# Projecting v of the four recurrent heads in one pass, tokens on partitions

## The chip, the cores and the metric

The kernel runs on one core of one Trainium2 chip. A core has the matrix engine TensorE (PE; the profile lists its weight loads separately as PEld), VectorE (DVE), ScalarE (ACT), GpSimd (POOL) and SyncE (SP, which here only issues transfers), 16 DMA engines, an on-chip memory of 128 partitions and eight PSUM banks into which PE writes. The metric is the device time of one execution in microseconds (us).

## The reference

The program is one layer of an encoder with 1024 tokens and 1024 channels: a mixer, a cross attention over 256 memory tokens, a mixture of 16 experts, and a final normalisation. The change lies in the mixer:

```
h = RMSNorm(x);  P = h @ W_in          # W_in is 1024 x 3584: seven slots of 512 columns
cb, cc, cx, hq, hf, hi, hg = split(P, 7)
y_a = cb * conv3_causal(cc * cx)
f = lb + (1 - lb) * sigmoid(hf);  k = (1 - lb) * sigmoid(-hf);  q = hq;  v = hi   # 4 heads of 128
S_t = diag(f_t) S_{t-1} + k_t v_t^T;   o_t = S_t^T q_t                            # per head
y_b = RMSNorm_per_head(o) * silu(hg)
x = x + concat(y_a, y_b) @ W_out
```

v is the slot `hi`: 512 columns, 128 for each of the four heads.

## The kernel before, in words

All products of this part are done in three matmuls on operands split into a high and a low part (`products`, L257 to L259: high by high, high by low, low by high), each with a 128x128 stationary operand and 512 streamed columns. The input x lies transposed (channels on partitions) as eight pairs `xh[k]`, `xl[k]` of 128x1024. W_in comes as 28 blocks of 128 columns; each block is a tile of 512 KB that holds the eight 128x128 pieces of its contraction.

A stream `W` brings the weights. It loads blocks in the order of `SEQ` through SP (L199) into free slots, and a generator `run` splits them: the high part by a cast on ACT (L163), the low part by a subtraction on DVE (L169). At most `W.limit` split blocks are ready ahead of their use. `W.get` forces a block that isn't ready. There are 48 slots of 128x1024, given out first in, first out.

`project(i, evac)` takes one block as the stationary operand and streams x: for each half of the tokens 8 triples of matmuls into one bank, which `evac` reads. Its result has the block's 128 channels on partitions and tokens along the free axis. After each triple it calls `advance(648)`. This is how the order of the program is written: `advance` moves a clock by 648 and runs the next step of every side generator whose due time has come; a generator gives its next due time by `yield`. `finish(s)` runs all remaining steps of a side at once. The steps are emitted in this order, and the compiler's scheduler, which has a cost model of its own, may start a later instruction first when the earlier one isn't ready by its model. On the chip each engine then runs its list in order.

The order is: `conv(0)` (blocks CC, CX, CB); then for each head h the inputs `hgrn_inputs(h)` with four projections HF, HI, HG, HQ, beside which the recurrent part `hgrn(h-1)` of the head before runs as a side; then `conv(1)` with three projections, beside `hgrn(3)`; then `conv(2)`, `conv(3)`, and the rest of the layer. After each `hgrn_inputs` and after `conv(1)` a `finish` completes the running head.

`hgrn` needs v with tokens on partitions. HI gives it with channels on partitions, copied out by ACT (L481). So `hgrn` begins with two steps: four PE transposes each (L264, called at L502), after which ACT copies four 128x128 tiles with the token's RMS factor `rx` as scale (L504). Then come the diagonal scores (L519), q times f (L525), seven levels of a doubling scheme (PE at L538 or L544; DVE at L547, L548, L550, L552), two steps that transpose k, two for the states (L581, L588), two for the outputs (L602, L604, squares on ACT at L608), the per-head RMS factor on POOL (`rstd_cols`, L180 and L181), its product with the output on DVE (L615), two steps that transpose the output (L264) and multiply by the gate on DVE (L623), and a store.

At the start `begin` computes `rx` and, by matmuls of ones with diagonal tiles (L387 on DVE, L390 on PE), a tile `rbc` of it along the free axis. Squares of x run on ACT (L372).

Of the kernel before, what the change touches and what calls it, by code (L numbers as in the profile page):

```python
# [14 lines left out]
AF = mybir.ActivationFunctionType  # L15
# [9 lines left out]
P = 128  # L25
T = 1024
D = 1024
NT = T // P
ND = D // P
HALF = 512  # L30
M = 256
NH = 4
# [53 lines left out]
def block_kernel(ctx: ExitStack, tc: tile.TileContext, A):  # L86
    nc = tc.nc
    act, dve, pool, pe, sp = nc.scalar, nc.vector, nc.gpsimd, nc.tensor, nc.sync
    HS = [slice(0, HALF), slice(HALF, T)]
    cut = lambda i: slice(i * P, (i + 1) * P)  # L90
# [3 lines left out]
    slots = Slots(ctx.enter_context(tc.tile_pool(name="slots", bufs=1)), "s", N_SLOTS, (P, T))  # L94
    banks = Slots(ctx.enter_context(tc.tile_pool(name="banks", bufs=1, space=PSUM)), "b", 8, (P, HALF))
# [12 lines left out]
    def side(gen, wait=0.0):  # L108
        s = [now[0] + wait, gen]
        sides.append(s)  # L110
        return s
# [140 lines left out]
    W = Stream()  # L252
# [8 lines left out]
    def transposes(src, half):  # L261
        pt = banks.get()
        for c in range(4):
            pe.transpose(pt[:, cut(c)], src[:, cut(half * 4 + c)], ident)  # L264
        spent(440)
        return pt
# [4 lines left out]
    CB, CC, CX, HQ, HF, HI, HG = 0, 4, 8, 12, 16, 20, 24  # L271
    SEQ = [CC, CX, CB]
    for h in range(4):
        SEQ += [HF + h, HI + h, HG + h, HQ + h]
    for j in range(1, 4):
        SEQ += [CC + j, CX + j, CB + j]

    xh, xl = [None] * ND, [None] * ND
# [33 lines left out]
    xs = [load_x(1)]  # L312
    load_w0(pieces[2])
    xs += [load_x(k) for k in range(2, ND)]
    for i in SEQ[2:]:
        W.add(("in", i), A["w_in"][i])
    split_w0(pieces[0])
    split_x(0, x0)
# [2 lines left out]
    for i in SEQ[:2]:  # L321
        w, hi, lo = w0[i]
# [18 lines left out]
    rx = const.tile([P, NT], F32, name="rx")  # L341
# [66 lines left out]
    def project(i, evac):  # L408

        W.get(("in", i))  # L410
        for hf in range(2):
            if i in started:
                ps = started[i][hf]
            else:
                ps = banks.get()
                for k in range(ND):
                    proj_mm(ps, i, k, hf)
                    advance(648)
            evac(hf, ps)
            banks.put(ps)  # L420
        W.drop(("in", i))
# [42 lines left out]
    def hgrn_inputs(h):  # L464
        c = slice(h, h + 1)
        z = slots.get()
        project(HF + h, lambda hf, ps: dve.tensor_tensor(z[:, HS[hf]], ps, rbc[:, HS[hf]], op=ALU.mult))
        f, k = slots.get(), slots.get()

        def gates():  # L470
            act.activation(f, z, AF.Sigmoid)
            yield 1300.0
            act.activation(k, z, AF.Sigmoid, scale=-1.0)
            slots.put(z)
            dve.tensor_scalar(f, f, oml[:, c], lb[:, c], op0=ALU.mult, op1=ALU.add)
            yield 1300.0
            dve.tensor_scalar(k, k, oml[:, c], None, op0=ALU.mult)

        fk = side(gates(), 700.0)
        vt = slots.get()  # L480
        project(HI + h, lambda hf, ps: act.copy(vt[:, HS[hf]], ps))  # L481
        finish(fk)
        gg, sg = slots.get(), slots.get()
        project(HG + h, lambda hf, ps: dve.tensor_tensor(gg[:, HS[hf]], ps, rbc[:, HS[hf]], op=ALU.mult))

        def silu():
            act.activation(sg, gg, AF.Sigmoid)
            yield 1300.0
            dve.tensor_tensor(gg, gg, sg, op=ALU.mult)
            slots.put(sg)  # L490

        gs = side(silu(), 700.0)
        q = slots.get()
        project(HQ + h, lambda hf, ps: dve.tensor_tensor(q[:, HS[hf]], ps, rbc[:, HS[hf]], op=ALU.mult))
        finish(gs)
        return f, k, q, vt, gg

    def hgrn(h, f, k, q, vt, gg):

        vn = slots.get()  # L500
        for hf in range(2):
            pt = transposes(vt, hf)  # L502
            for t in range(4):
                act.activation(vn[:, cut(hf * 4 + t)], pt[:, cut(t)], AF.Copy,  # L504
                               scale=rx[:, hf * 4 + t:hf * 4 + t + 1])
            banks.put(pt)
            yield 1300.0
        slots.put(vt)

# [1 line left out]
        sc, sb = slots.get(), half.get(F32, (P, NT * B32))  # L513
# [14 lines left out]
        tot = f  # L528
        for li, w in enumerate(LEVELS):
# [4 lines left out]
            for c in range(NT):  # L534
                if w < ALIGNED:
                    for b in range(4):
# [3 lines left out]
                                  start=True, stop=True)  # L540
# [25 lines left out]
            tot = nt_  # L566
# [10 lines left out]
        for hf in range(2):  # L577
            pv = banks.get()
            for c in range(4 - hf):
                cs = cut(hf * 4 + c)  # L580
                pe.matmul(pv[:, cut(c)], kn[:, cs], vn[:, cs], start=True, stop=True)  # L581
            spent(880)
            for c in range(4 - hf):
                i = hf * 4 + c
                if i == 0:
                    dve.tensor_copy(S[:, cut(0)], pv[:, cut(0)])
                else:
                    dve.scalar_tensor_tensor(S[:, cut(i)], S[:, cut(i - 1)], tot[:, i:i + 1], pv[:, cut(c)],  # L588
                                             op0=ALU.mult, op1=ALU.add)
            banks.put(pv)  # L590
            yield 1300.0
# [6 lines left out]
        for hf in range(2):  # L598
            po.append(banks.get())
            for c in range(4):  # L600
                i = hf * 4 + c
                pe.matmul(po[hf][:, cut(c)], sc[:, cut(i)], vn[:, cut(i)], start=True, stop=(i == 0))  # L602
                if i > 0:
                    pe.matmul(po[hf][:, cut(c)], q[:, cut(i)], S[:, cut(i - 1)], start=False, stop=True)  # L604
            spent(1750)
            for c in range(4):
                i = hf * 4 + c
                act.activation(on[:, cut(i)], po[hf][:, cut(c)], AF.Square, accum_out=sso[:, i:i + 1])  # L608
            yield 1300.0
        slots.put(sc, vn, q, S, tot)  # L610

        rstd_cols(ro, sso, P)
        yield 2600.0
# [18 lines left out]
    c0 = conv(0)  # L632
    finish(bs)
    side(c0)
    hs_ = None
    for h in range(4):
        st = hgrn_inputs(h)
# [854 lines left out]
def layout(inputs):  # L1492

    import numpy as np

    I = {k: np.asarray(v) for k, v in inputs.items()}
    c = np.ascontiguousarray
    f = np.float32
    x = I["x"][0]
    A = {"x": c(x), "xT": c(x.T.reshape(ND, P, T).transpose(1, 0, 2))}  # L1500
    cols = lambda v: np.asarray(v).reshape(-1, P).T
    A["vecs"] = c(np.concatenate([
        cols(I["mix_norm"][0]), cols(I["xattn_norm"][0]), cols(I["mem_norm"][0]), cols(I["ffn_norm"][0]),
        cols(I["conv_w"][0].reshape(-1)), cols(I["hgrn_lb"].reshape(-1)), cols(I["hgrn_norm"][0])], axis=1))
    A["w_in"] = c(I["w_in"][0].reshape(ND, P, 28, P).transpose(2, 1, 0, 3).reshape(28, P, T))
    A["mem"] = c(I["mem"][0])
    A["memT"] = c(I["mem"][0].T.reshape(ND, P, M).transpose(1, 0, 2))
    A["w_kv"] = c(I["w_kv"][0].reshape(ND, P, 16, P).transpose(2, 1, 0, 3).reshape(16, P, T))
    A["w_out"] = c(I["w_out"][0].reshape(4, 2, P, 2, HALF).transpose(3, 0, 2, 1, 4).reshape(2, 4, P, T))
    A["w_qT"] = c(I["w_q"][0].T.reshape(8, P, D))  # L1510
    A["w_o"] = c(I["w_o"][0].reshape(8, P, D))
    gu = [I[n][0].reshape(NE, ND, P, DE) for n in ("w_gate", "w_up")]
    A["w_gu"] = c(np.concatenate(gu, axis=3))
    A["ffn_norm"] = c(np.broadcast_to(I["ffn_norm"][0][None], (P, D)))
    A["w_dn"] = c(I["w_down"][0].reshape(NE, 4, P, D))
    A["final_norm"] = c(np.broadcast_to(I["final_norm"][None], (P, D)))
    rows = lambda v: np.broadcast_to(np.asarray(v, f), (P, len(v)))
    first = np.zeros((P, NE), f)
    first[0] = np.arange(NE) * T
    wr = np.concatenate([I["w_group"][0], np.zeros((D, 4), f), I["w_expert"][0]], axis=1)  # L1520
    never = f(-3.0e38)
    A["cst"] = c(np.concatenate([
        np.triu(np.ones((P, P), f), 1), rows(np.arange(P)), rows(np.arange(P) * P), first,
        np.arange(P, dtype=f)[:, None] + np.arange(NT, dtype=f) * P - T,
        np.arange(T, T + P, dtype=f)[:, None],
        rows(np.concatenate([I["b_group"][0], np.full(4, never), I["b_expert"][0]])),
        np.full((P, NT * 8), never), wr.reshape(ND, P, 24).transpose(1, 0, 2).reshape(P, ND * 24)], axis=1))
    A["ident"] = np.eye(P, dtype=f)
    mk = np.zeros((P, NM, B32 // 2), f)
    for li, w in enumerate(LEVELS[:NM]):  # L1530
        for j in range(B32 // 2):
            b0 = (j // w) * 2 * w
            for b in range(0, P, B32):
                mk[b + b0:b + b0 + w, li, j] = 1
    A["masks"] = mk
    return A
# [19 lines left out]
```

## Time and profile before

| | us |
|---|---|
| median of 3 runs (1220.21 to 1221.13) | 1221.01 |
| the profiled execution's own time | 1221.67 |
| its span, first to last instruction | 1219.9 |
| PE busy in the span | 1177.4 |
| ACT / DVE / POOL busy | 567.5 / 712.7 / 185.6 |

Times in rows count from the start of the span. A timeline row gives the start, the duration, the engine, the line, the operation, the operands (s a slot, b a bank, h a half slot), the count and, in brackets, how long the engine sat idle before and what released it. Matmuls overlap in the pipeline: the duration of one is longer than the distance to the next one's start. The mixer's four heads lie between 44 and 320 us.

### The profile page before, as it was taken

To read this page: it belongs to the slowest core of one execution; us is meant where nothing else is said; L and a number is where in the kernel's file an instruction comes from. 1 tells how busy PE (TensorE), PEld (TensorE's weight loads), DVE (VectorE), ACT (ScalarE), POOL (GpSimd) and SP (SyncE) were. 2 spreads that over 40 slices of the span, in tenths; PEclk is the share of its full clock that TensorE was granted. 3 is DMA by queue.
4 is the path that set the end of the run, shared out by engine and by line. 5 is a ranking of instruction groups with operands and counts; after the bars stand their busy time and mean duration, and the time that the engine had idled before them with its cause. 6 is when DMAs were issued, how large, how long until landed. Compare 5 with 4: busy or idle time off the path is not lost. (4 is left out here: it accounts for less than half of the span.)

```text
span 1219.9 us, 20586 instructions
## 1 busy us (share of the span) xinstructions
PE 1177.4 (97%) x7918; PEld 965.9 (79%) x7918; DVE 712.7 (58%) x1162; ACT 567.5 (47%) x965; POOL 185.6 (15%) x229
## 2 busy tenths in 40 slices
PE   9999999999999999999999999799999999999985
PEld 6787878787889988898888888678787777787762
DVE  6625454546358422374354776666867768668645
ACT  6613232323335402363244444455766767658633
POOL 1100101010100100200001334201222212122122
PEclk9999999999999999999999999899999999999998
DMA  9601110111426721130032331577979779798664
GB/s 342 243 18 41 48 55 35 37 53 53 157 87 232 275 80 35 35 104 1 1 108 82 134 110 70 186 265 242 317 244 373 263 258 350 249 351 288 244 175 203
DMA packets 58316, 196.48 MB, mean 161 GB/s; under 512 B 8925, under 2 KB 9565, under 8 KB 58208
## 3 DMA queue, kind: packets, MB, share of 16 engines
q1 hardware_dynamic: 45216, 157.69, 35.3%
q0 software_dynamic: 12704, 37.26, 10.4%
q8 instruction: 68, 1.11, 0.4%
q14 instruction: 40, 0.33, 0.1%
q10 hardware_dynamic: 288, 0.09, 0.0%
HBM read 173.49 MB, written 29.62 MB: 167 GB/s over the span
## 5 line engine op out<-in xcount | busy, mean ns | idle before, releaser
L257 PE MATMUL b<-s,s 128*128 128x512 f32 (+1 forms) x1056 | 402.8, 382 | 0.2 <-ACT s L165 0.2
L258 PE MATMUL b<-s,s 128*128 128x512 f32 (+1 forms) x1056 | 392.2, 371 | 0.4 <-DVE s L171 0.3
L259 PE MATMUL b<-s,s 128*128 128x512 f32 (+1 forms) x1056 | 392.5, 372 | 0.0
L169 DVE TENSOR_TENSOR s<-s,s 128x1024 fp32r<-128x1024 f32 (+2 forms) x272 | 315.2, 1204 | 53.6 <-ACT s L163 31.7
L163 ACT CAST s<-s 128x1024 fp32r<-128x1024 f32 (+2 forms) x272 | 268.5, 1042 | 130.3 <-PE b L259 48.0
L1124 PE MATMUL b<-s,s 128*128 128x512 f32 x1152 | 274.5, 396 | 6.6 <-ACT s L163 3.6
L1124 PEld LDWEIGHTS b<-s,s 128*128 128x128 f32 x1152 | 215.9, 190 | 54.0 <-ACT s L163 4.6
L259 PEld LDWEIGHTS b<-s,s 128*128 128x128 f32 x1056 | 199.0, 188 | 35.4 <-DVE s L169 0.3
L257 PEld LDWEIGHTS b<-s,s 128*128 128x128 f32 x1056 | 199.0, 189 | 32.9 <-ACT s L165 1.4
L258 PEld LDWEIGHTS b<-s,s 128*128 128x128 f32 x1056 | 199.5, 189 | 31.8 <-DVE s L171 1.6
L169 DVE TENSOR_TENSOR s<-b,s 128x512 fp32r<-128x512 f32 (+1 forms) x112 | 71.1, 648 | 47.6 <-ACT s L163 45.1
L1163 PE MATMUL b<-s,s 128*128 128x512 f32 x384 | 90.6, 391 | 0.0
L1199 POOL DMA_INDIRECT acd<-s,idi x30 | 57.0, 1901 | 203.7 <-DVE s L169 100.0
L1163 PEld LDWEIGHTS b<-s,s 128*128 128x128 f32 x384 | 71.6, 188 | 14.8
L163 ACT CAST s<-b 128x512 fp32r<-128x512 f32 (+1 forms) x112 | 60.8, 557 | 44.7 <-PE b L259 18.0
L1106 POOL DMA_INDIRECT s<-h3d,idi x32 | 36.0, 1126 | 107.9 <-PE b L1114 80.1
L1174 ACT COPY h<-b 64x512 f32<-64x512 f32 x32 | 18.6, 581 | 68.0 <-PE b L1163 57.0
L1175 DVE TENSOR_TENSOR h<-b,h 64x512 f32<-64x512 f32 x16 | 10.9, 683 | 63.1 <-ACT h L1174 63.1
L784 DVE TENSOR_TENSOR s<-b,s 128x512 f32<-128x512 f32 x16 | 11.1, 691 | 58.7 <-PE b L259 58.6
L264 PE MATMUL b<-ident,s 128*128 128x128 f32 x288 | 40.9, 273 | 1.0 <-DVE s L615 0.9
L547 DVE TENSOR_TENSOR s<-s,s 128x512 f32<-128x512 f32 x28 | 19.4, 691 | 38.2 <-PE b L538 21.9
L264 PEld LDWEIGHTS b<-ident,s 128*128 128x128 f32 x288 | 34.5, 140 | 8.0 <-DVE s L615 1.3
(232 smaller groups left out, 921.2 us busy)
## 6 DMA issues: line engine op xcount, KB each, us to landing
s<-in_w_gu_dram SPq DMA_DIRECT2D x128, 512.0 KB, 6.9
s<-in_w_dn_dram SPq DMA_DIRECT2D x64, 512.0 KB, 7.7
s<-in_w_in_dram SPq DMA_DIRECT2D x26, 512.0 KB, 3.6
s<-in_w_kv_dram SPq DMA_DIRECT2D x16, 512.0 KB, 5.3
h3d<-s POOLq DMA_DIRECT2D x9, 512.0 KB, 3.1
acd<-s POOLq DMA_DIRECT2D x9, 512.0 KB, 3.2
s<-in_xT_dram SPq DMA_DIRECT2D x16, 256.0 KB, 5.4
s<-in_x_dram SPq DMA_DIRECT2D x8, 512.0 KB, 8.6
```

What stands on the lines that cost most here:

```text
L163: act.copy(hi, src)
L169: (eng or dve).tensor_tensor(lo, src, hi.bitcast(F32), op=ALU.subtract)
L257: pe.matmul(ps, lh, rh, start=first, stop=False)
L258: pe.matmul(ps, lh, rl, start=False, stop=False)
L259: pe.matmul(ps, ll, rh, start=False, stop=last)
L264: pe.transpose(pt[:, cut(c)], src[:, cut(half * 4 + c)], ident)
L547: dve.tensor_tensor(k4[:, :, 0, :], k4[:, :, 0, :], tv[:, :, 1:2].to_broadcast([P, nb, w]), op=ALU.mult)
L1106: pool.indirect_dma_start(out=to, out_offset=None, in_=h3d, in_offset=rows, bounds_check=T - 1, oob_is_err=False)
L1124: pe.matmul(ps[n], l, r[:, HS[n]], start=a, stop=b)
L1163: pe.matmul(ps[n], l, r[:, HS[n]], start=first and i == 0, stop=last and i == 1)
L1174: act.copy(up2[UP], ps[UP])
L1199: pool.indirect_dma_start(out=acd, in_=src, in_offset=None, compute_op=ALU.add, out_offset=rows, bounds_check=T - 1, oob_is_err=False)
```

## The change

HI leaves the sequence of blocks; the columns of `hi` come instead as four tiles `w_v`, each with two contraction pieces of 128 rows and all 512 columns. A new function `values` runs between `conv(0)` and the first head: for each of the eight token tiles it makes 8 triples with x as the stationary operand and the four heads' weights streaming, and ACT copies the bank out with scale `rx`. The result, four tiles `vs`, has tokens on partitions; `hgrn` reads its head's columns from them. `hgrn_inputs` has three projections left, and the two transposing steps of `hgrn` are gone.

```diff
-        SEQ += [HF + h, HI + h, HG + h, HQ + h]
+        SEQ += [HF + h, HG + h, HQ + h]
...
-    for i in SEQ[2:]:
+    W.add(("in", SEQ[2]), A["w_in"][SEQ[2]])
+    for i in range(4):
+        W.add(("v", i), A["w_v"][i])
+    for i in SEQ[3:]:
         W.add(("in", i), A["w_in"][i])
...
         fk = side(gates(), 700.0)
-        vt = slots.get()
-        project(HI + h, lambda hf, ps: act.copy(vt[:, HS[hf]], ps))
         finish(fk)
...
-        vn = slots.get()
-        for hf in range(2):
-            pt = transposes(vt, hf)
-            for t in range(4):
-                act.activation(vn[:, cut(hf * 4 + t)], pt[:, cut(t)], AF.Copy,
-                               scale=rx[:, hf * 4 + t:hf * 4 + t + 1])
-            banks.put(pt)
-            yield 1300.0
-        slots.put(vt)
+    vs = []
+
+    def values():
+
+        w = [W.get(("v", i)) for i in range(4)]
+        vs.extend(slots.get() for _ in range(4))
+        for t in range(NT):
+            ps = banks.get()
+            for k in range(ND):
+                wh, wl = (w_[:, HS[k % 2]] for w_ in w[k // 2])
+                products(ps, xh[k][:, cut(t)], xl[k][:, cut(t)], wh, wl, k == 0, k == ND - 1)
+                advance(648)
+            act.activation(vs[t // 2][:, HS[t % 2]], ps, AF.Copy, scale=rx[:, t:t + 1])
+            banks.put(ps)
+        for i in range(4):
+            W.drop(("v", i))
+
+    def hgrn(h, f, k, q, gg):
+        vn = lambda c: vs[c // 2][:, c % 2 * HALF + h * P:c % 2 * HALF + (h + 1) * P]
...
-                pe.matmul(pv[:, cut(c)], kn[:, cs], vn[:, cs], start=True, stop=True)
+                pe.matmul(pv[:, cut(c)], kn[:, cs], vn(hf * 4 + c), start=True, stop=True)
...
-                pe.matmul(po[hf][:, cut(c)], sc[:, cut(i)], vn[:, cut(i)], start=True, stop=(i == 0))
+                pe.matmul(po[hf][:, cut(c)], sc[:, cut(i)], vn(i), start=True, stop=(i == 0))
...
     side(c0)
+    W.limit = 5
+    values()
+    W.limit = 3
```

## Rows read from the trace of the kernel before

**Rows 1.** The page: busy time of PE, its share of the span and its instructions; and the granted PE clock in 40 slices, in tenths of full speed.

```profile
PE 1177.4 (97%) x7918; PEld 965.9 (79%) x7918; DVE 712.7 (58%) x1162; ACT 567.5 (47%) x965; POOL 185.6 (15%) x229
...
PEclk9999999999999999999999999899999999999998
```

**Rows 2.** Busy time of each engine in stretches: the stretch, its length, then PE, PEld, DVE, ACT and POOL busy with the number of instructions, the granted PE clock, the DMA share and GB/s. The first is the first head's inputs, the next two are a head beside the next head's four projections, the last is the last head beside the three of `conv(1)`.

```profile
44.00:88.00 44.00, 44.00 (x193) 35.92 (x192) 21.58 (x25) 12.01 (x14) 1.59 (x2) 1.00 0.20 72
88.00:147.00 59.00, 59.00 (x695) 48.13 (x693) 27.64 (x48) 18.13 (x46) 2.82 (x3) 1.00 0.09 28
...
206.00:265.00 59.00, 59.00 (x696) 48.23 (x694) 31.02 (x55) 17.88 (x46) 3.41 (x4) 1.00 0.14 46
265.00:320.00 55.00, 54.12 (x673) 43.94 (x672) 34.09 (x52) 20.30 (x51) 5.20 (x8) 1.00 0.30 100
```

**Rows 3.** Waits of PE from 40 to 362 us: who waited for whom, us in total, times, the longest. The view has no other rows.

```profile
PE b L264 <- DVE s L615: 0.9, 1, 0.9
PE b L390 <- DVE s L387: 0.9, 1, 0.9
PE b L544 <- issue: 0.8, 1, 0.8
```

**Rows 4.** Instructions grouped by line, 0 to 420 us: count, busy us, mean ns of one, idle before.

```profile
L264 PE MATMUL b<-ident,s 128*128 128x128 f32 x96 | 14.0, 273 | 0.9 <-DVE s L615 0.9
...
L504 ACT ACTIVATE s<-b,rx 128x128 f32<-128x128 f32 x32 | 9.1, 368 | 39.9 <-PE b L264 39.9
...
L481 ACT COPY s<-b 128x512 f32<-128x512 f32 x8 | 4.7, 586 | 17.1 <-PE b L259 17.0
```

**Rows 5.** The instructions of L257 alone, the first of each triple, in two stretches of plain triples: length, PE busy with the count, PEld, clock, DMA. From 45 to 85 us weights are stationary and x streams; from 450 to 500 us (the output projection) activations are stationary and weights stream.

```profile
45.00:85.00 40.00, 23.11 (x59) 10.89 (x58) 1.00 0.22 79
450.00:500.00 50.00, 28.62 (x74) 13.77 (x74) 1.00 0.07 22
```

**Rows 6.** Timeline of PE about the two transposing steps of head 0; between the rows shown lie only matmuls of L257 to L259.

```profile
88.09 0.60 PE L264 MATMUL b<-ident,s 128*128 128x128 f32 x4
88.45 0.48 PE L257 MATMUL b<-s,s 128*128 128x512 f32 x1
88.76 0.39 PE L258 MATMUL b<-s,s 128*128 128x512 f32 x1
...
90.58 0.60 PE L264 MATMUL b<-ident,s 128*128 128x128 f32 x4
90.94 0.48 PE L257 MATMUL b<-s,s 128*128 128x512 f32 x1
91.25 0.40 PE L258 MATMUL b<-s,s 128*128 128x512 f32 x1
...
93.20 0.76 PE L519 MATMUL b<-s,s 128*32 128x32 f32 x64
```

**Rows 7.** Timeline of PE, POOL and DVE at the end of head 3, which stands beside three projections. From 311.94 to 315.70 lie 17 matmuls of L257 to L259.

```profile
311.79 0.39 PE L604 MATMUL b<-s,s 128*128 128x128 f32 x2
311.94 0.48 PE L257 MATMUL b<-s,s 128*128 128x512 f32 x1
...
313.64 0.54 POOL L459 DMA_DIRECT2D y_dram<-s  x1 [4.98 <-DVE s L457]
...
314.25 0.20 POOL L180 TENSOR_SCALAR ro<-sso 128x8 f32<-128x8 f32 x1
...
314.53 1.66 POOL L181 TENSOR_TENSOR ro<-ro,mhalf 128x8 f32<-128x8 f32 x1
...
315.70 0.39 PE L258 MATMUL b<-s,s 128*128 128x512 f32 x1
316.22 1.29 DVE L615 TENSOR_TENSOR s<-b,ro 128x512 f32<-128x512 f32 x2 [2.88 <-POOL ro L181]
...
316.97 0.66 PE L264 MATMUL b<-ident,s 128*128 128x128 f32 x4 [0.89 <-DVE s L615]
```

**Rows 8.** Timeline of PE and DVE at the boundary from head 0 to head 1 (the last matmul of HQ starts at 145.19).

```profile
145.19 0.39 PE L259 MATMUL b<-s,s 128*128 128x512 f32 x1
145.42 1.03 PE L264 MATMUL b<-ident,s 128*128 128x128 f32 x8
...
146.99 0.60 PE L264 MATMUL b<-ident,s 128*128 128x128 f32 x4
...
145.39 1.23 DVE L169 TENSOR_TENSOR s<-s,s 128x1024 fp32r<-128x1024 f32 x1 [2.19 <-PE b L258]
...
147.20 0.68 DVE L494 TENSOR_TENSOR s<-b,s 128x512 f32<-128x512 f32 x1
```

**Rows 9.** Timeline of PE and DVE about `conv(0)` and its end (an L169 row of x2 holds two blocks).

```profile
42.26 1.13 PE L390 MATMUL b<-s,ones 128*128 128x512 f32 x2 [0.87 <-DVE s L387]
...
44.81 0.80 PE L257 MATMUL b<-s,s 128*128 128x512 f32 x1
...
22.13 2.57 DVE L169 TENSOR_TENSOR s<-s,s 128x1024 fp32r<-128x1024 f32 x2 [0.85 <-ACT s L163]
...
42.71 1.22 DVE L169 TENSOR_TENSOR s<-s,s 128x1024 fp32r<-128x1024 f32 x1
...
44.04 2.36 DVE L169 TENSOR_TENSOR s<-s,s 128x1024 fp32r<-128x1024 f32 x2
46.31 1.22 DVE L444 TENSOR_TENSOR s<-s,s 128x1024 f32<-128x1024 f32 x1
```

More of the change, by code (lines that the diff above doesn't have):

```diff
@@ L495, in hgrn_inputs @@
         finish(gs)
-        return f, k, q, vt, gg
-    def hgrn(h, f, k, q, vt, gg):
-        vn = slots.get()
-        for hf in range(2):
-            pt = transposes(vt, hf)
-            for t in range(4):
-                act.activation(vn[:, cut(hf * 4 + t)], pt[:, cut(t)], AF.Copy,
-                               scale=rx[:, hf * 4 + t:hf * 4 + t + 1])
-            banks.put(pt)
-            yield 1300.0
-        slots.put(vt)
+        return f, k, q, gg
+    vs = []
[14 more added lines that the diff above has]
+        vn = lambda c: vs[c // 2][:, c % 2 * HALF + h * P:c % 2 * HALF + (h + 1) * P]
         sc, sb = slots.get(), half.get(F32, (P, NT * B32))
@@ L609, in hgrn @@
             yield 1300.0
-        slots.put(sc, vn, q, S, tot)
+        slots.put(sc, q, S, tot)
+        if h == NH - 1:
+            slots.put(*vs)
         rstd_cols(ro, sso, P)
@@ L1505, in layout @@
     A["w_in"] = c(I["w_in"][0].reshape(ND, P, 28, P).transpose(2, 1, 0, 3).reshape(28, P, T))
+    A["w_v"] = c(I["w_in"][0][:, 20 * P:24 * P].reshape(4, 2, P, HALF).transpose(0, 2, 1, 3).reshape(4, P, T))
     A["mem"] = c(I["mem"][0])
```

## The prediction, made before the changed kernel was run

> **What bounds the kernel now.** I read the page first. PE is busy for 97% of the span and its granted clock is at the upper level, 2.4 GHz, in nearly every slice [rows 1]. So only what takes time out of PE's list, or puts waits into it, can move the result; 1219.9 - 1177.4 = 42.5 us of PE idle time are spread over the whole kernel. Next, the stretches: through the four heads PE is busy 100% of the time but for about 0.8 and 0.9 us, while DVE stands at 47 to 62% and ACT below 37% [rows 2]. The list of PE's waits says the same from the other side: between 40 and 362 us PE waited three times, 2.6 us in all [rows 3]. The reader is to see that this part is a dense stream of matmuls into which the recurrence is threaded. Work removed from PE here is worth its issue time, no more, and whatever makes PE wait costs in full, because PE's list runs in order and the matmuls behind the waiting one stand too.
>
> A row's duration is not that issue time. Triples of plain matmuls come every 40/59 = 0.678 us, 0.226 us a matmul, though each lasts about 0.39 [rows 5].
>
> **The change part by part.**
>
> *The projection itself.* Before, four blocks HI make 4 x 2 x 8 triples; `values` makes 8 x 8. Both are 64 triples, 192 matmuls, of the same shape. The operand that is stationary is exchanged. The output projection already streams weights past stationary activations, at 50/74 = 0.676 us a triple against 0.678 [rows 5]. Cost: 0. The bytes loaded and the blocks split are as many as before.
>
> *The transposes.* Eight groups of four go (two per head). Four start within 88.45 - 88.09 = 0.36 us [rows 6], so 8 x 0.36 = 2.9 us. The matmul after each group is followed only 0.31 us later (88.45 to 88.76) where 0.226 is the rule: 0.085 lost at each resumption, 8 x 0.085 = 0.7 us. The longer step into L519 (93.20) stays. Gain on PE: 3.6 us, all on the path.
>
> Here a rule of the Trainium skill gives another sum. Its page "TensorE: Matmul & The Clock Gate", Part 4 (PE-mode transpose), says that a 128x128 transpose took about 275 ns in the context of a kernel. By it, 32 would be 8.8 us. The mean duration of L264 here agrees (273 ns, rows 4), but the distance of starts is 0.09 us each. I take the starts; the durations make a rival below.
>
> *ACT.* Eight copies L481 (4.7 us busy) and 32 scaled copies L504 (9.1 us) go [rows 4], and eight scaled copies of a whole bank come, by L481's row about 0.6 us each. ACT gains some 9 us and is idle for two thirds of this part, so that is worth 0.
>
> *The start of `values`.* All four v tiles are wanted within the first token tile, one per two triples, where HI, HG and HQ came 16 triples apart. Their loads take the places of HF0, HI0, HG0, HQ0 in SP's list; HF0 follows, with 64 triples in hand. Two blocks, CB and the place of the first v tile, were split from 22.13 on. The subtractions for the next three end at 43.93, 45.26 and 46.40 in the trace of before (42.71 + 1.22; two in 2.36 from 44.04) [rows 9]. PE spends its first six matmuls around the two L390 and goes on at 44.81; it needs the low part of the second tile at about 45.4, of the third at 46.6, of the fourth at 48. Each is over a microsecond early. If the scheduler lets one DVE operation of 1.22 us (L444, rows 9) in ahead, the last comes just in time. I take 0, at worst 1.2 us; a gain is excluded, since the wait at L390 hangs on `rx` and stays.
>
> *The end of each head.* This is where time can come back. By the code, a side step with `yield` 1300 or 1900 waits 3 triples, 2600 waits 5. Before, L519 came 7 triples after a head was handed over; now it comes after 1. From there: q times f, 6 triples to the first level, 7 levels of 3, two transposing steps, states, outputs: the second half of the outputs falls on triple 47, the POOL step on 50, its product on 55, the two transposes on 58 and 61. Three projections have 48 triples. So every head is cut short by `finish` with four steps left (POOL, L615, L264 twice); with four projections (64 triples) heads 0 to 2 had only the last transpose left. Head 3 before is the measured model: it stood beside three projections and had six steps left. The scheduler filled the gap with 17 matmuls of the next projection, then put L264 in, and PE waited for L615, which waited 2.88 us for POOL [rows 7]. 311.94 to 316.97 is 5.03 us; 17 x 0.226 = 3.84; price 1.2 us. That is the upper bound at each of the three new boundaries; the lower is 0, as the filling may suffice, and a gain is excluded because these boundaries had no wait [rows 3]. In head 3, POOL also had a store to issue first (L459 at 313.64), without which the factor could have started some 0.5 us earlier; heads 0 to 2 have no such store. I take 0.5 each: +1.5 us (0 to 3.6).
>
> Head 3 itself now has two steps fewer to finish, its factor ahead of that store: between -1.2 (its wait gone) and 0; I take -0.4.
>
> *L519 right behind q.* L519 needs q, whose second half DVE writes after the last matmul of HQ. At the boundary of heads 0 and 1 that ended at 147.20 + 0.68 = 147.88, while the first PE step of the new head started at 146.99 [rows 8]. Before, that step needed only v. Now it would be L519, 0.9 us too early, unless the scheduler places matmuls first. DVE was late there behind a subtraction (145.39, 1.23 us). Bounds 0 and 0.9, four times; no gain, since the step had no wait. As the scheduler knows of DVE, I take 0.2 each: +0.8 us (0 to 3.6). Behind a waiting L519 stand the next projection's matmuls only.
>
> *The denser levels.* The recurrence's DVE work is unchanged, beside 48 triples instead of 64. Head 3 before had this density (DVE 34.09 of 55, rows 2) without any wait of PE in its levels [rows 3]. I take 0; at worst one wait like that of L544 (0.8) in each of three heads, 2.4. Below nothing is excluded: the levels in heads 0 and 2 had no wait to lose. What hides DVE's latency between two levels is three triples, 2.0 us, as before.
>
> *Slots.* v holds four slots throughout instead of about two; the later parts get other slots. I find no place where the stream would starve; what it shifts in the rest I can't bound from these rows and put at 0.
>
> The sum: -3.6 + 1.5 - 0.4 + 0.8 = -1.7 us. Against the profiled execution's own 1221.67 (its span 1219.9 and 1.8 around) this is 1220.0. The median is 0.7 lower than that execution, so I forecast 1221.0 - 1.7 = 1219.3.
>
> **The rivals.**
>
> *A. Nothing is given back.* The scheduler fills all boundaries, head 3's wait goes: -3.6 - 1.2 = -4.8, 1216.2 us. For it: before, PE waited only once at such an end. Against: that one was just where the cover was short.
>
> *B. The recurrence no longer fits under three projections, and the change is slower.* At each boundary L264 stands for POOL and L615, and L519 for q. At the full prices: 3 x 1.2 + 4 x 0.9 - 3.6 = +3.6, 1224.6 us. It decides from 3.6 us of such waits on, 1.2 for each of the three boundaries; 2.0 each make it measurably slower. For it: 61 triples wanted, 48 there, and head 3's row. Against: all the prices would have to be paid in full, and the extra store on POOL isn't there.
>
> *C. The gain is swallowed later.* The earlier end of the mixer shows, but the 42.5 us of idle PE elsewhere grow by as much, as the loads of the later parts keep their pace: 1221.0. Against: PE is busy without a break up to 361 us and 97% overall.
>
> *D. The transposes were worth their durations*, by the skill's figure or by L264's mean of 273 ns: 32 x 0.273 = 8.7, with nothing returned 1212.3 us. Against: starts 0.09 us apart [rows 6].
>
> **How the numbers follow.** Forecast 62%, A 14%, B 12%, C 8%, D 4%. What a measurement of this kernel can tell from no change is about 0.2%, 2.4 us: faster is below 1218.6, slower above 1223.4. The forecast's own spread (give-backs from 0.5 to 4 us, 1217.8 to 1221.5) lies about a third below 1218.6, which makes 20 of its 62%. Faster: 20 + 14 + 4 = 38%. Slower: B's upper part and a little of the rest, 11%. The same: 51%. The range reaches from near A, 1216.5, to most of the way to B, 1223.2; D and B's end are left out.
>
> **What would show it.** L264 with 64 matmuls instead of 96 and L504 gone; 192 matmuls in a row after `conv(0)`, some 43.5 us, without a PE wait above a few tenths; a head about 59 - 10.8 - 0.9 = 47 us (the stretch of rows 2 without 48 matmuls and two groups of transposes). The step into `values` is wrong if PE waits for a cast or a subtraction there. In PE's waits, L264 for L615 should stand three or four times with 0.2 to 1 us, L519 for L494 with 0 to 0.5. If their sum passes 3.6, B holds; if it is near 0 and the time is 1216, A. If the kernel's first 361 us shrink and the total does not, C.

## The result, and the profile after

The changed kernel takes 1227.8 us in the median of four runs (1226.7 to 1230.6), the kernel before 1220.6 (1220.1 to 1221.1): a ratio of 1.0057, 95% interval 1.0045 to 1.0070. It is slower by 7 us. The forecast was 1219.3, its range ended at 1223.2, and the rival that came nearest, B, said 1224.6.

The page's busy time of PE and its granted clock, to be held against [rows 1]:

```profile
PE 1175.6 (96%) x7886; PEld 964.1 (79%) x7886; DVE 712.1 (58%) x1162; ACT 559.0 (46%) x933; POOL 186.4 (15%) x229
...
PEclk9999999999999999999999999899999999999988
```

PE has 32 instructions and 1.8 us of busy time fewer, in a span that is 5.5 us longer. So the transposes did go, and more than they were worth came back as idle time. Grouped by line, 0 to 420 us, what [rows 4] showed of the transposes and of v's copies reads now:

```profile
L264 PE MATMUL b<-ident,s 128*128 128x128 f32 x64 | 10.7, 294 | 7.7 <-DVE s L626 7.7
...
L511 ACT ACTIVATE s<-b,rx 128x512 f32<-128x512 f32 x8 | 5.5, 690 | 27.5 <-PE b L259 27.5
```

64 transposes instead of 96, and one scaled copy of a bank per token tile instead of four small ones. But PE sat idle 7.7 us in front of those 64, where it was 0.9 before. (Lines have moved: L615, the product with the per-head factor on DVE, is L626 now; L519, L538, L602, L604, L608 are L528, L547, L611, L613, L617.) PE's waits from 40 to 367 us are two rows, against [rows 3]:

```profile
PE b L264 <- DVE s L626: 7.7, 4, 2.0
PE b L393 <- DVE s L390: 0.9, 1, 0.9
```

Neither the start of `values` nor L519 (L528) nor a level of the recurrence appears. Four waits, one at each head's end, and one of 0.9 us that was there before are all there is. The stretches of the heads, columns as in [rows 2], show the same, and a second thing in the column behind POOL's, the granted clock:

```profile
121.00:168.00 47.00, 45.46 (x617) 36.84 (x615) 24.19 (x44) 12.47 (x34) 2.82 (x3) 1.00 0.11 35
168.00:215.00 47.00, 46.53 (x582) 37.87 (x582) 27.93 (x50) 13.43 (x35) 1.56 (x2) 1.00 0.10 35
215.00:262.00 47.00, 45.00 (x612) 36.17 (x611) 27.89 (x50) 13.41 (x29) 2.45 (x3) 0.96 0.14 47
262.00:316.00 54.00, 52.16 (x659) 42.60 (x659) 28.14 (x48) 15.02 (x42) 4.10 (x5) 0.97 0.15 51
```

PE misses 1.5, 0.5, 2.0 and 1.8 us (the first wait lies across the first two stretches; the fourth comes behind them, from 318 to 320 us), and in two of them its clock isn't whole any more. One boundary, head 0 to head 1, in the timeline of all engines:

```profile
164.07 0.39 PE L613 MATMUL b<-s,s 128*128 128x128 f32 x2
164.22 0.47 PE L257 MATMUL b<-s,s 128*128 128x512 f32 x1
...
165.42 0.22 ACT L617 ACTIVATION_READ_ACCUMULATOR s<-b 128x1 f32 x1
...
165.74 0.19 POOL L180 TENSOR_SCALAR ro<-sso 128x8 f32<-128x8 f32 x1 [9.76 <-ACT s L617]
165.78 0.68 PE L528 MATMUL b<-s,s 128*32 128x32 f32 x54
166.02 1.68 POOL L181 TENSOR_TENSOR ro<-ro,mhalf 128x8 f32<-128x8 f32 x1
167.72 1.29 DVE L626 TENSOR_TENSOR s<-b,ro 128x512 f32<-128x512 f32 x2 [1.84 <-POOL ro L181]
168.47 0.66 PE L264 MATMUL b<-ident,s 128*128 128x128 f32 x4 [2.01 <-DVE s L626]
```

After the last output matmul (164.07) PE's list holds six matmuls of the next projection (HF of head 2), 54 of the 64 small ones of L528 (the diagonal scores of head 1), and then L264. The way from that output to L264's operand goes over ACT (to 165.64), POOL (to 167.70) and DVE (first half at about 168.4): 4.4 us. The list covers 2.4 of them. Behind L264 stand the rest of L528 and of HF's matmuls, none of which needs what L264 waits for. The Trainium skill, "TensorE: Matmul & The Clock Gate", Part 2, says that of PE's queue only weight loads are pulled ahead while matmuls stay in program order; the gap here, with the rest of a projection standing behind L264, agrees.

To compare kernels apart from the start and from the later stages, take the way from the second pair of the matmuls that spread `rx` (L393, after `conv(0)`) to L707, behind the heads and `conv(2)`. PE's timeline in the changed kernel:

```profile
43.11 1.10 PE L393 MATMUL b<-s,ones 128*128 128x512 f32 x2
...
366.18 0.59 PE L707 MATMUL b<-dg,ones 128*128 128x256 f32 x2
```

and in the kernel before:

```profile
44.28 1.10 PE L390 MATMUL b<-s,ones 128*128 128x512 f32 x2
...
361.00 0.59 PE L693 MATMUL b<-dg,ones 128*128 128x256 f32 x2
```

That is 323.1 us against 316.7, 6.4 us more. From there to the end of the span both need 859 us (1225.4 - 366.2 and 1219.9 - 361.0). So nothing was swallowed later (rival C), and nothing was lost there either: in these two profiles the whole loss lies in the heads.

### The profile page after: what moved, and what is told of

It reads as the page before. It is cut to its first block, busy times and chain, and to the rows that moved or that the text cites. A ratio compares the mean times of both kernels' runs of the same rounds, so it can differ in the third digit from the quotient of the medians.

```text
span 1225.4 us, 20466 instructions
## 1 busy us (share of the span) xinstructions
PE 1175.6 (96%) x7886; PEld 964.1 (79%) x7886; DVE 712.1 (58%) x1162; ACT 559.0 (46%) x933; POOL 186.4 (15%) x229
## 5 line engine op out<-in xcount | busy, mean ns | idle before, releaser
L257 PE MATMUL b<-s,s 128*128 128x512 f32 (+1 forms) x1056 | 402.6, 382 | 0.4 <-ACT s L163 0.3
L259 PE MATMUL b<-s,s 128*128 128x512 f32 (+1 forms) x1056 | 393.6, 373 | 0.0
L169 DVE TENSOR_TENSOR s<-s,s 128x1024 fp32r<-128x1024 f32 (+2 forms) x272 | 315.0, 1202 | 81.0 <-ACT s L163 48.9
L259 PEld LDWEIGHTS b<-s,s 128*128 128x128 f32 x1056 | 199.7, 189 | 35.5 <-DVE s L169 0.3
L257 PEld LDWEIGHTS b<-s,s 128*128 128x128 f32 x1056 | 199.6, 189 | 33.1 <-ACT s L165 0.7
L169 DVE TENSOR_TENSOR s<-b,s 128x512 fp32r<-128x512 f32 (+1 forms) x112 | 71.0, 647 | 47.3 <-ACT s L163 44.2
L264 PE MATMUL b<-ident,s 128*128 128x128 f32 x256 | 37.6, 278 | 7.8 <-DVE s L626 7.7
L264 PEld LDWEIGHTS b<-ident,s 128*128 128x128 f32 x256 | 31.1, 142 | 14.2 <-DVE s L626 8.6
L861 ACT ACTIVATE s<-b,mx,r 128x256 f32<-128x256 f32 x32 | 17.8, 561 | 46.2 <-DVE mx L859 46.2
```

The costliest lines, as they stand in the source:

```text
L169: (eng or dve).tensor_tensor(lo, src, hi.bitcast(F32), op=ALU.subtract)
L257: pe.matmul(ps, lh, rh, start=first, stop=False)
L259: pe.matmul(ps, ll, rh, start=False, stop=last)
L861: act.activation(pb[:, h * M:(h + 1) * M], ps[:, (h % 2) * M:(h % 2 + 1) * M], AF.Exp, scale=r, bias=mx[:, h:h + 1], accum_out=sm[:, h:h + 1])
```

## The experiments

The theory after this reading, called P in the expectations: with three projections instead of four as cover, `finish` hands a head's last four steps to the scheduler at once. It places L264 behind too few matmuls, and PE pays for the difference and for what its clock does afterwards. Rival F: the new form of v, or its slots, costs. Rival D: the recurrence is too dense for DVE and ACT beside three projections.

The kernels, with the time, the ratio to the kernel before with its interval, the way in the heads as defined above, and PE's waits at L264:

| kernel | median us | ratio | heads us | waits at L264 us |
|---|---|---|---|---|
| before (1220.6 to 1220.9 beside the others) | 1220.6 | 1 | 316.7 | 0.9 |
| changed | 1227.8 | 1.0057 (1.0045 to 1.0070) | 323.1 | 7.7 in 4 |
| e1_tail | 1216.7 | 0.9965 (0.9952 to 0.9977) | 311.6 | none |
| e2_ahead | 1228.7 | 1.0062 (1.0045 to 1.0078) | 322.9 | 6.2 in 4 |
| e3_nopow | 1214.0 | 0.9948 (0.9931 to 0.9965) | 313.4 | 0.9 in 3 |
| e4_before_tail | 1220.0 | 0.9991 (0.9982 to 1.0001) | 315.2 | none |
| e6_store | 1220.4 | 0.9996 (0.9986 to 1.0006) | 318.0 | 1.7 |
| e8_again (changed, unedited) | 1229.4 | 1.0069 (1.0052 to 1.0086) | 324.8 | 7.7 in 4 |

**e1_tail: the head's last steps keep their due times.**

```diff
     for h in range(4):
         st = hgrn_inputs(h)
-        if hs_ is not None:
-            finish(hs_)
         hs_ = side(hgrn(h, *st))
     side(conv(1))
-    finish(hs_)
     W.limit = 6
-    side(conv(2))
+    c2 = conv(2)
+    finish(hs_)
+    side(c2)
```

> The changed kernel, but the recurrent part of a head is no longer finished at the end of the next head's inputs: its last four steps (factor on POOL, product on DVE, two transposing steps) keep their due times and run beside the next projections. Theory P (the ends of the heads: the transposes are put into PE's list some 2 us before POOL and DVE are done, and PE waits and loses its clock): the four waits of L264 for the product on DVE (7.7 us) fall below 0.5 us in all, no clock below full speed in the heads, and the time is 1215 to 1217 us, 0.3 to 0.5% below the kernel before. Rival F (the new form of v itself costs, or its slots): 1225 us or more, as in the changed kernel. Rival D (the recurrence beside three projections is too dense for DVE and ACT): waits move into the levels, above 1221 us.

It takes 1216.7 us, inside what P said, 4 us below the kernel before and 11 below the changed one. PE's waits from 40 to 360 us are one row:

```profile
PE b L393 <- DVE s L390: 0.9, 1, 0.9
```

and the boundary of heads 0 and 1 reads, in the timeline of PE, POOL and DVE:

```profile
164.55 0.39 PE L613 MATMUL b<-s,s 128*128 128x128 f32 x2
...
166.50 1.68 POOL L181 TENSOR_TENSOR ro<-ro,mhalf 128x8 f32<-128x8 f32 x1
...
168.21 1.29 DVE L626 TENSOR_TENSOR s<-b,ro 128x512 f32<-128x512 f32 x2 [1.48 <-POOL ro L181]
...
172.23 0.73 PE L547 MATMUL b<-s,s 128*32 128x16 f32 x64
...
173.69 0.60 PE L264 MATMUL b<-ident,s 128*128 128x128 f32 x4
```

POOL and DVE do the same at the same distance from L613 as in the changed kernel. DVE still stands 1.5 us for POOL, and it costs nothing. L264 now comes 9 us after L613, among the next head's levels (L547), over 4 us after the first half of its operand is ready. F and D fall: the form of v, its slots and the density of heads 0 to 2 are those of the changed kernel. (Head 3 ends beside `conv(2)` here, so it has three projections more.)

**e2_ahead: the kernel before, with HI moved ahead in its old form.**

```diff
+    SEQ += [HI + h for h in range(4)]
     for h in range(4):
-        SEQ += [HF + h, HI + h, HG + h, HQ + h]
+        SEQ += [HF + h, HG + h, HQ + h]
...
-        vt = slots.get()
-        project(HI + h, lambda hf, ps: act.copy(vt[:, HS[hf]], ps))
         finish(fk)
...
     side(c0)
+    vts = []
+    for h in range(4):
+        vt = slots.get()
+        project(HI + h, lambda hf, ps: act.copy(vt[:, HS[hf]], ps))
+        vts.append(vt)
```

> The kernel before, with its four HI projections moved ahead of the heads in their old form, transposes and all. Theory P: the same short cover, so PE waits at the four ends of the heads, 1 to 2 us each, its clock falls behind some of them, and the transposes are still paid: 1225 to 1232 us. Rival F: no change from the kernel before, 1219.5 to 1221.5 us.

1228.7 us: the move alone, without the new form, makes the kernel as slow as the change does. PE's waits from 40 to 368 us:

```profile
PE b L264 <- DVE s L614: 6.2, 4, 1.9
PE b L543 <- issue: 1.0, 1, 1.0
PE b L391 <- DVE s L388: 0.9, 1, 0.9
```

Its four waits are 1.71, 1.70, 1.88 and 0.88 us. The shortest is head 3's, the only one whose factor stands behind a store in POOL's list. The clock did not fall behind any of them in this profile, which P had expected behind some. In the heads this kernel is 6.2 us above the one before: 5.3 us more of waits at L264, 0.2 more at L543, and three more restarts of the matmul stream. A restart is put at about 0.2 us, an estimate: idle time counts from the end of the last matmul, and in the dense stream the next one starts 0.16 us before that end (0.39 less 0.226, [rows 5]). That the sum comes so near to the changed kernel's 6.4 is chance: here the transposes are still paid and the clock held, there it is the other way round.

**e3_nopow: the changed kernel without the power in the factor.**

```diff
-        rstd_cols(ro, sso, P)
+        pool.tensor_scalar(ro, sso, 1.0 / P, EPS, op0=ALU.mult, op1=ALU.add)
```

> The changed kernel without the power in the per-head factor (POOL, 1.68 us; the factor is then the mean square plus epsilon and not its inverse root). Theory P with POOL as the part that the scheduler's model misses: the four waits fall from 1.9 to 0.2 to 0.4 us each, the clock holds, 1216 to 1219 us. If the squares on ACT or the product on DVE are what is missed, the list of PE moves with the factor and waits of over 1 us stay: 1223 us or more. Rivals F and D: 1225 us or more.

The heads take 313.4 us, 9.6 less than in the changed kernel, the waits 0.9 us together. (The total, 1214.0 against 1216 to 1219 expected, isn't used: the later stages, which ran on other values here, took 853.5 us instead of 859, and no run shows why.) The boundary of heads 0 and 1 on POOL, PE and DVE:

```profile
165.53 0.19 POOL L623 TENSOR_SCALAR ro<-sso 128x8 f32<-128x8 f32 x1 [9.76 <-ACT s L617]
165.58 0.68 PE L528 MATMUL b<-s,s 128*32 128x32 f32 x54
165.76 1.29 DVE L626 TENSOR_TENSOR s<-b,ro 128x512 f32<-128x512 f32 x2
...
166.50 0.66 PE L264 MATMUL b<-ident,s 128*128 128x128 f32 x4 [0.25 <-DVE s L626]
```

What follows is in the count: 54 matmuls of L528 stand before L264, exactly as with the power. (At the end of head 2 it is 62, where it was 64 and one of L257.) The scheduler put L264 in the same place whether POOL had 1.68 us more to do or not, so its model gives that power next to nothing. The wait fell from 2.01 to 0.25, by the power's duration and the 0.1 us to the next engine.

**e4_before_tail: the kernel before with e1_tail's edit.**

> The kernel before with the same edit as e1_tail: a head's last steps keep their due times. Theory P: only the one wait of head 3 (0.9 us and the restart) was there to go, so 1219 to 1220.5 us; e1_tail lies 3 to 4 us below it, which is what the 32 transposes cost on PE. Rival F: e1_tail lies above this kernel. Rival D: the two lie within 1 us.

1220.0 us, a ratio of 0.9991 to the kernel before with an interval that reaches 1: by the time alone this is no difference. In the heads it is 1.6 us shorter, with head 3's wait gone and also the 0.8 us at L544 in [rows 3], which P had not counted. The use of this kernel is the comparison with e1_tail, since neither has a wait at L264. PE's timeline in e4_before_tail and then in e1_tail:

```profile
42.74 1.10 PE L390 MATMUL b<-s,ones 128*128 128x512 f32 x2
...
357.89 0.59 PE L692 MATMUL b<-dg,ones 128*128 128x256 f32 x2
```

```profile
43.59 1.10 PE L393 MATMUL b<-s,ones 128*128 128x512 f32 x2
...
355.23 0.59 PE L706 MATMUL b<-dg,ones 128*128 128x256 f32 x2
```

315.15 against 311.64: v in one pass without transposes is worth 3.5 us where nothing waits at L264 (medians: 3.3).

**e6_store: the kernel before, with the convolution's stores on ACT's queue.** This asks why head 3's end, from which the prediction took its price, was cheaper than the new boundaries.

```diff
-            pool.dma_start(y_dram[j], cv)
+            act.dma_start(y_dram[j], cv)
```

> The kernel before, with the stores of the convolution's results issued by ACT instead of POOL. At head 3's end POOL's list then holds no store ahead of the factor, as at the ends of heads 0 to 2 in the changed kernel. If the scheduler counts that store when it decides how many matmuls to put before L264 (17 in the kernel before), fewer stand there now, 10 or 11, and PE's one wait rises from 0.9 to 1.6 to 1.9 us: the whole of the forecast's error at the ends of the heads. If the store only delayed the factor on the chip, as the prediction had it, the wait falls to 0.2 to 0.5 us. Time: 1220 to 1223 us in the first case, 1219.5 to 1220.5 in the second.

The end of head 3 on PE and POOL, against [rows 7]:

```profile
311.10 0.39 PE L604 MATMUL b<-s,s 128*128 128x128 f32 x2
311.24 0.48 PE L257 MATMUL b<-s,s 128*128 128x512 f32 x1
...
312.76 0.20 POOL L180 TENSOR_SCALAR ro<-sso 128x8 f32<-128x8 f32 x1 [4.78 <-ACT s L608]
...
313.41 0.40 PE L257 MATMUL b<-s,s 128*128 128x512 f32 x1
...
315.49 0.66 PE L264 MATMUL b<-ident,s 128*128 128x128 f32 x4 [1.67 <-DVE s L615]
```

From 311.24 to 313.41 lie ten matmuls, where there were 17, and the wait is 1.67 us instead of 0.89. The scheduler does count the store, and it had put seven matmuls more in for it: 7 x 0.226 = 1.6 us of cover. The store itself had delayed the factor by only 0.8 us (2.46 us from the last L604 to L180 before, 1.66 now), and 1.6 - 0.8 is what the wait grew by. From the last output matmul to L264 it is 4.4 us here as in the changed kernel; the list covers 2.7 of them, against 2.4 there, which is the rest of the way to 2.0. The total didn't move (ratio 0.9996), though the heads took 1.3 us more; a difference of that size isn't told by the times.

**e8_again: the changed kernel, unedited.**

> The changed kernel once more, unedited, for a second profile. The four waits of L264 have their length from the lists of instructions and stay at 1.8 to 2.0 us each, 7.7 in all. Whether the clock falls behind a wait varies from one execution to the next: in the first profile it fell behind two of the four. If that is what spreads the times of this kernel (1226.7 to 1230.6), a profile with more falls has a longer stretch of the four heads at the same waits, some 1.5 us for each. 1226.5 to 1230.5 us.

The same four waits, to within 0.02 us each, and another time: 324.8 us in the heads instead of 323.1. The granted clock (the column behind POOL's) behind the first three waits, which end at 168.32, 219.37 and 270.87:

```profile
170.00:173.00 3.00, 3.00 (x10) 2.42 (x9) 2.58 (x5) 0.00 (x0) 0.61 (x1) 0.51 0.08 33
222.00:225.00 3.00, 3.00 (x10) 2.33 (x9) 2.29 (x5) 0.00 (x0) 0.59 (x1) 0.65 0.42 175
273.00:276.00 3.00, 3.00 (x10) 2.38 (x9) 2.63 (x5) 0.00 (x0) 0.61 (x1) 0.61 0.42 175
```

Three falls here. In the first profile of the changed kernel the first wait passed without one and the second had one:

```profile
170.00:174.00 4.00, 4.00 (x21) 3.29 (x19) 3.11 (x6) 0.00 (x0) 0.61 (x1) 1.00 0.32 131
...
219.00:222.00 3.00, 3.00 (x10) 2.45 (x10) 2.41 (x5) 0.00 (x0) 0.59 (x1) 0.50 0.00 0
```

The third had one as well (0.50 from 271 to 273 us).

What a fall costs can be read from the same piece of the list at either level. Behind waits one and two stand the same instructions up to the first level (L547): two groups of four transposes, the last ten of L528, and 21 matmuls of L257 to L259. In the first profile:

```profile
168.47 0.66 PE L264 MATMUL b<-ident,s 128*128 128x128 f32 x4 [2.01 <-DVE s L626]
...
174.75 0.74 PE L547 MATMUL b<-s,s 128*32 128x16 f32 x64
...
217.91 0.66 PE L264 MATMUL b<-ident,s 128*128 128x128 f32 x4 [2.00 <-DVE s L626]
...
225.78 0.74 PE L547 MATMUL b<-s,s 128*32 128x16 f32 x64
```

and in e8_again behind wait one:

```profile
168.32 0.66 PE L264 MATMUL b<-ident,s 128*128 128x128 f32 x4 [2.00 <-DVE s L626]
...
176.19 0.74 PE L547 MATMUL b<-s,s 128*32 128x16 f32 x64
```

174.75 - 168.47 = 6.3 us at 2.4 GHz throughout; 225.78 - 217.91 and 176.19 - 168.32 are 7.9, where the clock fell to 1.2 GHz about a microsecond after PE had started again: 1.6 us a fall. One fall more in e8_again goes with 1.8 us more in the heads at equal waits, near enough.

Behind the fourth wait, at the end of head 3, the clock stayed whole in both profiles (1.00 from 320 to 324 us in the first, and from 322 to 326 in e8_again). There 11 matmuls of 512 columns stand ahead of the waiting L264, and no L528:

```profile
317.64 0.39 PE L257 MATMUL b<-s,s 128*128 128x512 f32 x1
317.87 0.39 PE L258 MATMUL b<-s,s 128*128 128x512 f32 x1
320.08 0.66 PE L264 MATMUL b<-ident,s 128*128 128x128 f32 x4 [1.83 <-DVE s L626]
```

The account of the changed kernel's 323.1 against e1_tail's 311.6, 11.4 us: waits 7.7, two falls of the clock 3.2, and four restarts of the stream at some 0.2; that is 11.7. Against the kernel before, +6.4: transposes -3.5, waits +6.8, clock +3.2, three more restarts +0.6, less the wait at L544 (0.8) that the kernel before happened to have; that is 6.3.

## Why the prediction was wrong

- **The frame was right.** PE bounds this part; the transposes were worth their issue time, and the waits cost in full and, with the clock, more. The stages behind the heads didn't change.
- **The transposes were right.** Forecast 3.6 us, 3.5 by e1_tail against e4_before_tail; put down to the 32 transposes alone, that is 0.11 us each. The figure of about 275 ns in the Trainium skill's page "TensorE: Matmul & The Clock Gate", Part 4, is a duration (of a bf16 transpose there; 273 ns for f32 here); as a price it gave 8.8 in the prediction's estimate, and rival D rested on it. The measurement decides for the distance of starts.
- **The projection, the start of `values`, L519 and the levels.** Costs of 0, 0, 0.8 and 0 were put in; none of them shows a wait. From the second L393 to the first L528 stand 333 matmuls, what is left of `values` and the first head's projections, without a gap. The 0.8 for L519 was too much: the scheduler put six matmuls ahead of it where one triple stood in the order, and PE did not wait.
- **The end of each head is the step that failed.** The prediction had the place, the chain (squares, POOL, L615, L264) and the arithmetic of 48 against 61 triples. It had the size wrong: 0.5 us at each of three boundaries, 1.2 at most. Measured were waits of 2.0, 2.0 and 1.8 us, and a restart of about 0.2 each. For all four ends together the sum had +1.1 us (1.5 less the 0.4 of head 3); waits, restarts and clock came to +10.6 against the kernel before. It also argued in the wrong direction from the row that it took its price from. Head 3's end had a store on POOL, and the prediction said that the boundaries without one would be cheaper. The store was in the scheduler's model as well, and it was the reason for seven of the 17 matmuls in front of L264. e6_store shows it: without the store the wait goes from 0.89 to 1.67 us. A row with an extra instruction in it bounds the case without it only if the planner that laid out the list didn't see that instruction.
- **Head 3 itself** was to gain 0.4. It lost 0.9 (1.83 instead of 0.89): the factor now stands ahead of the store in POOL's list, and 11 matmuls stand in front of L264 instead of 17, near the ten of e6_store.
- **The clock was not in the sum at all.** Before, no fall stood behind the one wait at a head's end. Behind the four waits near 2 us there were two falls in one profile and three in the other, 1.6 us each where it could be measured.
- **Rival B** named the wait at the heads' ends, at 12%, and was the nearest in time, but not for the reasons in its sum. Half of its give-back, 3.6 us, was L519 standing for q, which never happened; the other half, 3 x 1.2, had the same price from head 3's row and was too low; the clock was missing there too.

Settled by the runs: the loss is in the position of HI's projections (e2_ahead), it is the wait at the four ends (e1_tail), and the part of the chain that the list doesn't cover is the power on POOL (e3_nopow). Open: why the clock falls behind some of these waits and not behind others of the same length. All five falls stand behind waits of L264 that follow the small matmuls of L528 (directly at the ends of heads 0 and 1, with one matmul of L257 between at the end of head 2); there were six such waits in the two profiles of the changed kernel. Behind the eight waits of L264 with large matmuls ahead of it (head 3 in both profiles, 1.83; four of 0.88 to 1.88 in e2_ahead; 1.67 in e6_store; 0.89 before) there was none. That speaks for a part of L528 in it, but no run moved L528 alone, and one wait behind L528 passed without a fall.

The version to keep is e1_tail: the changed kernel without the `finish` at the end of each `hgrn_inputs`, and with the last one moved behind the projections of `conv(2)`, 0.35% below the kernel before (0.23 to 0.48%).

## What to carry to other kernels

Work that looks like a plain cost on the bound engine may also be the cover for somebody else's latency. Before moving it, count what runs beside it, in the units in which the order is written, and see which steps fall into a forced finish. Where a scheduler with its own cost model lays out an in-order list, a wait is the real latency less what the list has put in front. Take the latency from the durations of the chain itself (here 1.1 on ACT, 1.9 on POOL, 0.7 on DVE, with the hand-overs 4.4 us), and the cover from a list that was laid out around the same instructions, not from a neighbouring case whose list was laid out around something else. Spacing the steps further apart, as the due times did in e1_tail, left no wait for the model to misjudge.

## What the runs showed of the hardware that had not been expected

PE idle for 1.8 to 2.0 us in an otherwise dense stream was followed by the lower clock in five of eight cases (1.2 GHz, granted 0.50 from 219 to 222 us), and where the same piece of the list was seen at both levels a fall cost another 1.6 us, four fifths of the wait itself. All five had the small matmuls of L528 just ahead of the wait. Behind four waits of 0.9 to 1.9 us in e2_ahead and one of 1.7 in e6_store, with large matmuls ahead, it did not fall. Whether the falls also spread the times isn't shown: four runs of the changed kernel lie 3.9 us apart and four more 2.8, but the kernel before, 1.1 over its first four, reached 2.9 over 13; one pair of profiles, with two and three falls, is all that was seen of it.
